# A gated layer's output phase in another order of blocks, its mixes one product later, the next rows' splits later

## The chip, the cores and the metric

The program runs on one core of a Trainium2 chip, and the metric is the device time of one execution in microseconds. TensorE does the matrix products, VectorE (DVE) and ScalarE (ACT) the elementwise work, GpSimd (POOL) helps in the first layer, SyncE (SP) issues most DMA transfers.

## What is computed

A decoder trunk of two layers on x (1 x 2048 x 1024, float32). Layer 0 is a hybrid of dilated sliding-window and differential attention; the change leaves it as it is. Layer 1 is a chunked gated MLP:

```python
def sgu_layer(x, norm_g, w_in, ln_g, ln_b, w_s, b_s, w_out):
    h = rms_norm(x, norm_g)                       # 2048 x 1024
    u, v, g = split(h @ w_in)                     # three times 2048 columns
    u = gelu(u)
    v = layer_norm(gelu(v), ln_g, ln_b)
    # in each 128-row chunk n and each of 8 column groups: causal 128 x 128 product
    sp = einsum('gts,bnsgc->bntgc', tril(w_s), chunks(v)) + b_s
    y = u * sp * silu(g)
    return x + y @ w_out                          # 2048 x 2048 by 2048 x 1024
```

## The kernel before

The 16 chunks of 128 rows ("blocks") of layer 1 go through in four groups `gi` of four. A group's blocks 0 to 3 are taken as two rows j = 0, 1 by two row halves r (block j + 2r). Every projection is a Strassen-like scheme (`strassen`, L915): seven products for j = 0 and j = 1 each, 14 steps n, and each step is twelve matmuls of 128x512 (L925): four slices of the inner dimension by three terms, since each float32 operand is held as a high and a low part in the faster float32r format. The helper `split` (L91, L92) makes these parts: ScalarE copies the high part, VectorE subtracts to get the low one. All such splits of weights (`w`), rows (`h`), mixed rows and turned rows (both `vs`) have line L92.

A group runs so:

1. v (m = 1) for both column halves `cc`, with GELU and the statistics of the layer norm.
2. For each `cc`: u (m = 0). During its steps the `mix` generators are called, eight of them, one for each row, row half r and column half c. The first call normalises a piece of v and splits it (`vs`, a ring of four); the second does the spatial products, six matmuls (L1095 to L1097) into a bank of `pp` (there are two), and ScalarE adds the bias into `vv`. u's own product with it waits in the list `pend`.
3. Then the gate g (m = 2). `g_done` (L1126) makes the gated columns: tanh on ScalarE (L1129), two operations on VectorE (L1130, L1131); L1131 writes them into `vv`.
4. Then the output phase (L1150 on): 16 output products M0 to M15 over (c, h, block), where h is a half of the 1024 output columns. `turned(b, c)` (L1133) transposes four 128x128 tiles (L1137) into `pp` and splits them into `vs`; twelve matmuls (L1168 to L1170) use them in one of three accumulator banks `y`; VectorE adds the bank to `acc` (L1171), and in the second column half the sum goes out.

Weights come in through `slot` (L860): SyncE loads a raw tile `wr` (a ring of three), which is split into one of five `w2` tiles. Some tiles of u's products (`k` 1 and 3) are split once, stored, and loaded again in the groups behind by L867 (`ws`).

While the output phase of `cc == 1` runs, the next group's rows are prepared (`rows_sums`, L962): a load of four row tiles into `hr` (one buffer, L969), then splits and sums (L979 to L995) for block pair 0 (j = 0), then, with the same buffer, for pair 1. Beside the output products of group 0, `cc == 0`, `turn` (L1000) finishes the last two blocks of layer 0, with transposes into the same `pp` (its multiply is L1014).

What sets the order: TensorE's instructions stand in the order in which the program is written. The other engines' instructions are ordered by a list scheduler that simulates the program; each engine then takes them in that order. So the place of a call in the text decides TensorE's order, and elsewhere only what the scheduler makes of it.

Of the kernel before, what the change touches and what calls it, by code (L numbers as in the profile page):

```python
# [60 lines left out]
def _trunk(tc, a, out):  # L61
# [3 lines left out]
    with ExitStack() as top:  # L65
# [760 lines left out]
        with ExitStack() as st:  # L826
            w1 = st.enter_context(tc.tile_pool(name="D_w", bufs=1, reuse_waits="tile"))
            ps = st.enter_context(tc.tile_pool(name="D_ps", bufs=1, space=PSUM, reuse_waits="tile"))
            NG, GB = 4, 4
# [5 lines left out]
            def tile_(shape, dt, tag, bufs):  # L835
                got = ahead.pop(tag, None)
                return w1.tile(shape, dt, name=tag, tag=tag, bufs=bufs) if got is None else got

            def psum(tag, shape, bufs):
                got = ahead_ps.pop(tag, None)  # L840
                return ps.tile(shape, F32, name=tag, tag=tag, bufs=bufs) if got is None else got
# [73 lines left out]
            def strassen(ht, m, cc, sum_to, done):  # L915


                x, y, u2, o = {}, {}, {}, {}

                def product(j, acc, i, w, start):  # L920

                    z = ht[j][i]
                    for kc in range(4):
                        for k, (p, q) in enumerate(((0, 0), (0, 1), (1, 0))):
                            T.matmul(acc, z[:, p, kc], w[kc][q], start=start and kc == k == 0, stop=kc == 3 and k == 2,  # L925
                                     skip_group_check=True)

                def taken(j, r, c, p):
                    o[j] = sum_to(j, r, c)
                    A.copy(o[j], p)  # L930

                def summed(j, r, c, p, q=None):
                    z = sum_to(j, r, c) if q is not None else o[j]
                    V.tensor_add(z, p, z if q is None else q)
                    done(j, r, c, z)

                for n, (i, *which) in enumerate(PRODUCTS):
                    w = quarter(m, cc, *which)
                    for j in range(2):
                        if n == 0:  # L940
                            x[j] = psum("x", [P, 512], 3)
                        elif n in (1, 3):
                            y[j] = psum("y", [P, 512], 3)
                        product(j, x[j] if n in (0, 2, 4, 6) else y[j], i, w, n in (0, 1, 3))
                        if n == 0:
                            taken(j, 0, 0, x[j])
                        elif n == 1:
                            summed(j, 0, 0, y[j])
                        elif n == 2:
                            u2[j] = tile_([P, 512], F32, "u2", 2)  # L950
                            A.copy(u2[j], x[j])
                        elif n == 3:
                            taken(j, 1, 1, y[j])
                        elif n == 4:
                            summed(j, 1, 1, x[j])
                        elif n == 5:
                            summed(j, 0, 1, y[j], u2[j])
                        elif n == 6:
                            done(j, 1, 0, x[j])
                        yield  # L960
# [63 lines left out]
            for g in rows:  # L1024
                next(g)
            for gi in range(NG):
                blocks = range(GB * gi, GB * gi + GB)
                vv, st6, acc = {}, {}, {}
                ht = ready.pop(gi)
                for b in blocks:  # L1030
# [6 lines left out]
                def columns(cc, c):  # L1037
                    return slice(512 * cc + 1024 * c, 512 * cc + 1024 * c + 512)
# [32 lines left out]
                for cc in range(2):  # L1071
# [43 lines left out]
                    mixes = [mix(*z) for z in order]  # L1115
                    pend = []
                    for n, _ in enumerate(strassen(ht, 0, cc, new_sum, u_done)):
                        if 3 <= n < 11:
                            next(mixes[n - 3], None)
                        if 1 <= n < 9:  # L1120
                            next(mixes[n - 1])
                        while pend and pend[0][0] <= n - 3:
                            pend.pop(0)[1]()


# [7 lines left out]
                    def turned(b, c):  # L1133
                        pt = psum("pp", [P, 512], 2).rearrange("p (c t) -> p c t", t=P)
                        s0 = columns(cc, c).start
                        for i in range(4):
                            T.transpose(pt[:, i], vv[b][:, s0 + P * i:s0 + P * i + P], ident)  # L1137
                        yT = tile_([P, 2, 512], F32R, "vs", VS_BUFS).rearrange("p k (c t) -> p k c t", t=P)
                        split(yT[:, 0], yT[:, 1], pt)
                        return yT  # L1140

                    for n, _ in enumerate(strassen(ht, 2, cc, new_sum, g_done)):
                        if n == 12:
                            nxt = turned(blocks[0], 0)

                    todo = iter(())
                    if cc == 1 and gi + 1 < NG:
                        ready[gi + 1] = []
                        todo = steps([rows_sums(gi + 1, j) for j in range(2)])
                    seq = [(c, h, b) for c in range(2) for h in range(2) for b in blocks]  # L1150
                    yT = {blocks[0]: nxt}
                    for n, (c, h, b) in enumerate(seq):
                        es = slice(512 * h, 512 * h + 512)
                        if n % GB == 0:
                            k0 = columns(cc, c).start // P
                            wo2 = []
                            for k in range(0, 4, 2):
                                wo2 += slot(wout[:, k0 + k:k0 + k + 2, es], 2)

                        if n + 1 < len(seq) and seq[n + 1][1] == 0:  # L1160
                            yT[seq[n + 1][2]] = turned(seq[n + 1][2], seq[n + 1][0])
                        if cc == 0 and c == h == 0:
                            acc[b] = tile_([P, D], F32, "acc", GB)
                            with tc.issue_after(urgent.ins):
                                nc.sync.dma_start(acc[b], x1_s[b])
                        po = psum("y", [P, 512], 3)
                        for i in range(4):
                            T.matmul(po, yT[b][:, 0, i], wo2[i][0], start=i == 0, stop=False)  # L1168
                            T.matmul(po, yT[b][:, 0, i], wo2[i][1], start=False, stop=False)  # L1169
                            T.matmul(po, yT[b][:, 1, i], wo2[i][0], start=False, stop=i == 3)  # L1170
                        V.tensor_add(acc[b][:, es], po, acc[b][:, es])  # L1171
                        if cc == 1 and c == 1:
                            nc.sync.dma_start(out[b * P:(b + 1) * P, es], acc[b][:, es])
                        if gi == 0 and cc == 0 and n in (6, 10):
                            turn(NB - LATE + n // 8)
                        next(todo, None)


def _host_constants():
# [56 lines left out]
```

## Time and profile before

| | |
|---|---|
| median of 3 runs | 3186.36 us (3172.94 to 3189.53) |
| profiled execution, and its span | 3193.26 us; 3191.5 us |
| mean granted TensorE clock | 0.979 of full |
| TensorE (PE) busy | 3001.6 us, 94% of the span |
| VectorE (DVE) busy | 2142.9 us, 67% |
| ScalarE (ACT) busy | 1641.5 us, 51% |
| GpSimd (POOL) busy | 726.6 us, 23%, none of it in the last half |

Layer 1 takes the last 1368 us of the span. A busy share is an average over stages that have different limits: what a change is worth in one stage is to be read from the waits in that stage. In rows of the trace a bracket such as `[1.34 <-DVE vs L92]` says that the engine stood idle 1.34 us before this instruction, until VectorE's instruction of line 92 on the tile `vs` was done; `x4` is a run of four like instructions, and the time before the engine's name is how long they took.

### The profile page before, as it was taken

To read this page: it belongs to the slowest core of one execution; us is meant where nothing else is said; L and a number is where in the kernel's file an instruction comes from. 1 tells how busy PE (TensorE), PEld (TensorE's weight loads), DVE (VectorE), ACT (ScalarE), POOL (GpSimd) and SP (SyncE) were. 2 spreads that over 40 slices of the span, in tenths; PEclk is the share of its full clock that TensorE was granted. 3 is DMA by queue.
4 is the path that set the end of the run, shared out by engine and by line. 5 is a ranking of instruction groups with operands and counts; after the bars stand their busy time and mean duration, and the time that the engine had idled before them with its cause. 6 is when DMAs were issued, how large, how long until landed. Compare 5 with 4: busy or idle time off the path is not lost.

```text
span 3191.5 us, 45535 instructions
## 1 busy us (share of the span) xinstructions
PE 3001.6 (94%) x15240; PEld 2508.5 (79%) x15240; DVE 2142.9 (67%) x4822; ACT 1641.5 (51%) x3012; POOL 726.6 (23%) x1855
## 2 busy tenths in 40 slices
PE   7879899998989999998999989999998999999999
PEld 6668787887878778887887778778887888777887
DVE  5436686457855677556886787757767677757765
ACT  5535555455545555554454664635554553645553
POOL 5535443445334543442123000000000000000000
PEclk9989999999999999999999999999999999999999
DMA  9987967878587876758437774647554664547553
GB/s 343 334 248 228 267 205 226 252 218 261 194 249 222 242 239 202 215 159 231 149 129 255 234 235 159 209 156 251 167 161 153 200 236 144 177 145 245 164 170 107
DMA packets 379915, 668.75 MB, mean 210 GB/s; under 512 B 61856, under 2 KB 176672, under 8 KB 375584
## 3 DMA queue, kind: packets, MB, share of 16 engines
q1 hardware_dynamic: 351648, 568.04, 57.9%
q0 software_dynamic: 27456, 95.70, 8.3%
q8 instruction: 120, 1.97, 0.3%
q10 hardware_dynamic: 576, 2.10, 0.2%
q14 instruction: 115, 0.94, 0.1%
HBM read 506.08 MB, written 134.48 MB: 201 GB/s over the span
## 4 chain that ended last, share of the span: by engine, by line
PE 72%; DMA 11%; DVE 9%; issue 3%; ACT 3%; POOL 1%; SPq 1%; DVEq 0%; ACTq 0%; POOLq 0%
PE x L925 14%; PE y L925 11%; PE pm L326 5%; PE pm L328 5%; PE pm L327 5%; PE pu L549 3%; PE y L1170 3%; PE y L1168 3%; PE y L1169 3%; PE po L645 3%; PE s_ps L506 3%; DMA hT<-hts 2%; DMA tq<-in_sgu_w_in 2%; PE pT L525 2%; PE sd_ps L608 1%
## 5 line engine op out<-in xcount | busy, mean ns | idle before, releaser
L92 DVE TENSOR_TENSOR w<-wr,w 128x1024 fp32r<-128x1024 f32 x376 | 459.3, 1222 | 240.2 <-ACT w L92 239.3
L925 PE MATMUL x<-w,h 128*128 128x512 f32 x2304 | 558.9, 397 | 9.7 <-DVE w L92 5.6
L925 PEld LDWEIGHTS x<-w,h 128*128 128x128 f32 x2304 | 434.1, 190 | 110.5 <-DVE w L92 8.2
L326 PE MATMUL pm<-wh,hT 128*128 128x512 f32 x1024 | 453.7, 443 | 69.0 <-DMA hT<-hts 51.1
L92 ACT CAST w<-wr 128x1024 fp32r<-128x1024 f32 x376 | 394.2, 1049 | 235.1 <-PE y L1170 89.8
L925 PE MATMUL y<-w,h 128*128 128x512 f32 x1728 | 414.1, 394 | 0.0
L327 PE MATMUL pm<-wl,hT 128*128 128x512 f32 x1024 | 410.6, 401 | 2.7 <-POOL wl L92 2.6
L328 PE MATMUL pm<-wh,hT 128*128 128x512 f32 x1024 | 411.9, 402 | 0.0
L925 PEld LDWEIGHTS y<-w,h 128*128 128x128 f32 x1728 | 323.3, 188 | 71.5
L326 PEld LDWEIGHTS pm<-wh,hT 128*128 128x128 f32 x1024 | 200.3, 196 | 92.5 <-issue 41.4
L615 ACT ACTIVATE sd<-sd,nmd 128x128 f32<-128x128 f32 (+15 forms) x128 | 153.9, 1203 | 165.8 <-DVE nmd L611 163.9
L328 PEld LDWEIGHTS pm<-wh,hT 128*128 128x128 f32 x1024 | 197.1, 192 | 46.2 <-DVE hT L217 1.2
L1170 PE MATMUL y<-w,vs 128*128 128x512 f32 x512 | 205.6, 401 | 11.8 <-DVE vs L92 11.7
L327 PEld LDWEIGHTS pm<-wl,hT 128*128 128x128 f32 x1024 | 199.9, 195 | 21.1 <-POOL wl L92 4.8
L1168 PE MATMUL y<-w,vs 128*128 128x512 f32 x512 | 209.7, 409 | 0.5 <-ACT vs L92 0.5
L1169 PE MATMUL y<-w,vs 128*128 128x512 f32 x512 | 204.3, 399 | 0.0
L517 ACT ACTIVATE sm<-sm,um 128x256 f32<-128x256 f32 (+1 forms) x256 | 115.5, 486 | 157.0 <-DVE um L515 156.8
L549 PEld LDWEIGHTS pu<-vt,pTs 128*128 128x128 f32 x1200 | 160.0, 192 | 22.3 <-ACT um L552 5.5
L549 PE MATMUL pu<-vt,pTs 128*128 128x65 f32 x1200 | 156.5, 268 | 6.3 <-ACT um L552 3.5
L515 DVE CUSTOM_DVE_ANT_0 sm<-s_ps,masks 128x256 f32<-128x256 f32 (+1 forms) x224 | 84.6, 415 | 110.8 <-PE s_ps L506 110.6
L645 PEld LDWEIGHTS po<-vd,pTds 128*128 128x128 f32 x1088 | 145.9, 192 | 15.0 <-ACT pTds L653 1.6
L1171 DVE TENSOR_TENSOR acc<-y,acc 128x512 f32<-128x512 f32 x128 | 88.2, 689 | 94.0 <-PE y L1170 92.6
(220 smaller groups left out, 5855.8 us busy)
## 6 DMA issues: line engine op xcount, KB each, us to landing
hT<-hts SPq DMA_DIRECT2D x224, 512.0 KB, 4.5
wr<-t SPq DMA_DIRECT2D x168, 512.0 KB, 4.3
wr<-in_sgu_w_in SPq DMA_DIRECT2D x144, 512.0 KB, 4.4
wr<-in_sgu_w_out SPq DMA_DIRECT2D x64, 512.0 KB, 3.9
tq<-in_sgu_w_in SPq DMA_DIRECT2D x96, 256.0 KB, 4.2
t<-tq POOLq DMA_DIRECT2D x48, 512.0 KB, 4.9
w<-ws SPq DMA_DIRECT2D x24, 1024.0 KB, 5.8
hts<-hT SPq DMA_DIRECT2D x32, 512.0 KB, 7.1
```

The costliest lines, as they stand in the source:

```text
L92: return A.copy(hi, src), E.tensor_sub(lo, src, hi.bitcast(F32))
L326: T.matmul(pm, z[:, 0, k], w[dc][0], start=dc == 0, stop=False)
L327: T.matmul(pm, z[:, 0, k], w[dc][1], start=False, stop=False)
L328: T.matmul(pm, z[:, 1, k], w[dc][0], start=False, stop=dc == DC - 1)
L517: A.activation(sm[:, t, :w], sm[:, t, :w], AF.Exp, bias=nm, scale=-1.0)
L549: T.matmul(pu[:, g0 % 4 + t], pTs[:, t, P * q:P * q + P], vt[pat][:, vb, 65 * i:65 * i + 65], start=q == 0, stop=q == nk - 1)
L615: A.activation(sm[:, :L], sm[:, :L], AF.Exp, bias=nm[:, nch - 1:nch], scale=-1.0, accum_out=lsum)
L645: T.matmul(po, pTs[:, k], v[:, k4 + k], start=k4 + k == 0, stop=k4 + k == i)
L925: T.matmul(acc, z[:, p, kc], w[kc][q], start=start and kc == k == 0, stop=kc == 3 and k == 2, skip_group_check=True)
L1168: T.matmul(po, yT[b][:, 0, i], wo2[i][0], start=i == 0, stop=False)
L1169: T.matmul(po, yT[b][:, 0, i], wo2[i][1], start=False, stop=False)
L1170: T.matmul(po, yT[b][:, 1, i], wo2[i][0], start=False, stop=i == 3)
```

## The change

Four things change in layer 1, and nothing in what is computed but the order in which float32 sums are added:

- The output phase takes the column halves as c = 1, 0 and the blocks as 2, 3, 0, 1. The stores of the second column half therefore go with c = 0.
- Its first two turned blocks are called at steps 12 and 13 of the gate's scheme; each later one after the add of the output product two places ahead of its own, where before it was called ahead of the matmuls of the product one place ahead.
- The spatial products of the mixes are called one step later (4 to 11 for 3 to 10), and so are the products in `pend`.
- The steps of the next group's rows are taken two at a time from n = 6 on, where before one was taken after each n.

```diff
-                        if 3 <= n < 11:
-                            next(mixes[n - 3], None)
+                        if 4 <= n < 12:
+                            next(mixes[n - 4], None)
                         if 1 <= n < 9:
                             next(mixes[n - 1])
-                        while pend and pend[0][0] <= n - 3:
+                        while pend and pend[0][0] <= n - 4:
                             pend.pop(0)[1]()
...
+                    yT = {}
                     for n, _ in enumerate(strassen(ht, 2, cc, new_sum, g_done)):
-                        if n == 12:
-                            nxt = turned(blocks[0], 0)
+                        if n >= 12:
+                            b = blocks[n - 10]
+                            yT[b] = turned(b, 1)
...
-                    seq = [(c, h, b) for c in range(2) for h in range(2) for b in blocks]
-                    yT = {blocks[0]: nxt}
+                    seq = [(c, h, b) for c in (1, 0) for h in range(2) for b in blocks[2:] + blocks[:2]]
...
-                        if n + 1 < len(seq) and seq[n + 1][1] == 0:
-                            yT[seq[n + 1][2]] = turned(seq[n + 1][2], seq[n + 1][0])
-                        if cc == 0 and c == h == 0:
+                        if cc == 0 and n < GB:
                             acc[b] = tile_([P, D], F32, "acc", GB)
...
                         V.tensor_add(acc[b][:, es], po, acc[b][:, es])
-                        if cc == 1 and c == 1:
+
+                        if n + 2 < len(seq) and seq[n + 2][1] == 0:
+                            yT[seq[n + 2][2]] = turned(seq[n + 2][2], seq[n + 2][0])
+                        if cc == 1 and c == 0:
                             nc.sync.dma_start(out[b * P:(b + 1) * P, es], acc[b][:, es])
                         if gi == 0 and cc == 0 and n in (6, 10):
                             turn(NB - LATE + n // 8)
-                        next(todo, None)
+                        if n > 5:
+                            next(todo, None)
+                            next(todo, None)
```

How this moves instructions, in three places. First TensorE, group 1, from the last gate products into the output phase of `cc == 1`, before (`vv_22623`, `22625`, `22627` and `22629` are the group's blocks 0 to 3; `L925` with `w_24897` and `w_24902` are the last two steps of the gate's scheme):

```order
L925 MATMUL x<-w_24897,h_22276 128x512 x6
L925 MATMUL x<-w_24902,h_22276 128x512 x6
L1137 MATMUL pp<-ident,vv_22623 128x128 x4
L925 MATMUL x<-w_24897,h_22416 128x512 x6
L925 MATMUL x<-w_24902,h_22416 128x512 x6
L1137 MATMUL pp<-ident,vv_22625 128x128 x4
L1168 MATMUL y<-w_24947,vs 128x512
...
L1137 MATMUL pp<-ident,vv_22627 128x128 x4
```

The same place in the changed kernel:

```order
L925 MATMUL x<-w_24897,h_22394 128x512 x6
L925 MATMUL x<-w_24902,h_22394 128x512 x6
L1137 MATMUL pp<-ident,vv_22627 128x128 x4
L925 MATMUL x<-w_24897,h_22502 128x512 x6
L925 MATMUL x<-w_24902,h_22502 128x512 x6
L1137 MATMUL pp<-ident,vv_22629 128x128 x4
L1167 MATMUL y<-w_24955,vs 128x512
...
L1137 MATMUL pp<-ident,vv_22623 128x128 x4
```

The transposes stand at the same places; the blocks in them are others. Next VectorE in the same phase, from the split of the second turned block on, before (`h` is the next group's rows; from `h_25122` on it is block pair 1):

```order
L92 TENSOR_TENSOR vs<-pp,vs 128x512
L1130 SCALAR_TENSOR_TENSOR th<-th,x 128x512
L92 TENSOR_TENSOR h_24987<-hr,h_24987 128x512
L1171 TENSOR_TENSOR acc<-y,acc 128x512
L1130 SCALAR_TENSOR_TENSOR th<-th,x 128x512
L1131 TENSOR_TENSOR vv_22627<-vv_22627,th 128x512
L1131 TENSOR_TENSOR vv_22629<-vv_22629,th 128x512
L92 TENSOR_TENSOR h_25122<-hr,h_25122 128x512
L92 TENSOR_TENSOR h_25123<-hr,h_25123 128x512
L986 TENSOR_TENSOR ct<-hr 128x512
L92 TENSOR_TENSOR vs<-pp,vs 128x512
```

And in the changed kernel (`h_25208` begins pair 1):

```order
L92 TENSOR_TENSOR vs<-pp,vs 128x512
L1130 SCALAR_TENSOR_TENSOR th<-th,x 128x512
L92 TENSOR_TENSOR h_25105<-hr,h_25105 128x512
L1130 SCALAR_TENSOR_TENSOR th<-th,x 128x512
L1170 TENSOR_TENSOR acc<-y,acc 128x512
L92 TENSOR_TENSOR vs<-pp,vs 128x512
L1131 TENSOR_TENSOR vv_22627<-vv_22627,th 128x512
L1131 TENSOR_TENSOR vv_22629<-vv_22629,th 128x512
L1170 TENSOR_TENSOR acc<-y,acc 128x512
L92 TENSOR_TENSOR vs<-pp,vs 128x512
L92 TENSOR_TENSOR h_25208<-hr,h_25208 128x512
L92 TENSOR_TENSOR h_25209<-hr,h_25209 128x512
```

Two splits of turned blocks and one more add now stand ahead of the first split of pair 1; the last split of pair 0 (`h_24987`, `h_25105`) stands where it stood. Last TensorE at the first mix of group 0 and `cc == 0`, before (`w_20501` and `w_20508` are the weights of step 4):

```order
L925 MATMUL y<-w_20440,h_19745 128x512 x6
L925 MATMUL y<-w_20445,h_19745 128x512 x6
L1095 MATMUL pp<-vs,wsp 128x256
L1096 MATMUL pp<-vs,wsp 128x256
L1097 MATMUL pp<-vs,wsp 128x256
...
L925 MATMUL x<-w_20501,h_19723 128x512 x6
L925 MATMUL x<-w_20508,h_19723 128x512 x6
```

And in the changed kernel:

```order
L925 MATMUL y<-w_20440,h_19745 128x512 x6
L925 MATMUL y<-w_20445,h_19745 128x512 x6
L925 MATMUL x<-w_20492,h_19723 128x512 x6
L925 MATMUL x<-w_20499,h_19723 128x512 x6
L1095 MATMUL pp<-vs,wsp 128x256
L1096 MATMUL pp<-vs,wsp 128x256
L1097 MATMUL pp<-vs,wsp 128x256
```

Step 4 of u's scheme has moved ahead of the first mix.

## Rows read from the trace of the kernel before

**Rows 1.** The head of the page.

```profile
span 3191.5 us, 45535 instructions
```

**Rows 2.** Waits of TensorE from 1824 us on: us in total, times, longest us.

```profile
PE pp L1137 <- DVE vv L1131: 17.3, 3, 5.8
PE y L1170 <- DVE vs L92: 11.7, 12, 1.7
PE pp L1096 <- DVE vs L92: 6.0, 4, 1.8
...
PE pp L1137 <- DVE th L1014: 0.5, 1, 0.5
```

**Rows 3.** Windows, second output phase, groups 0 to 3: us; busy (x) by engine (PE, PEld, DVE, ACT, POOL); clock.

```profile
2067.63:2101.48 33.85, 23.71 (x98) 17.91 (x97) 24.68 (x37) 11.22 (x18) 0.00 (x0) 0.90 0.40 135
2424.05:2457.32 33.27, 24.36 (x98) 18.53 (x97) 24.68 (x37) 11.22 (x18) 0.00 (x0) 0.90 0.41 139
2781.91:2814.93 33.02, 24.27 (x98) 18.84 (x97) 24.67 (x37) 11.31 (x18) 0.00 (x0) 0.90 0.33 107
3139.22:3160.69 21.47, 21.11 (x98) 16.94 (x96) 12.82 (x17) 5.29 (x7) 0.00 (x0) 1.00 0.16 56
```

**Rows 4.** Timeline of TensorE, group 1, that phase: start us, us, instruction [idle before <- releaser].

```profile
2426.46 0.50 PE L1170 MATMUL y<-w,vs 128*128 128x512 f32 x1 [1.34 <-DVE vs L92]
...
2428.66 0.40 PE L1170 MATMUL y<-w,vs 128*128 128x512 f32 x1
2434.82 1.09 PE L1137 MATMUL pp<-ident,vv 128*128 128x128 f32 x4 [5.76 <-DVE vv L1131]
...
2440.55 0.60 PE L1137 MATMUL pp<-ident,vv 128*128 128x128 f32 x4
```

**Rows 5.** Timeline of VectorE, the same stretch.

```profile
2423.91 0.69 DVE L1131 TENSOR_TENSOR vv<-vv,th 128x512 f32<-128x512 f32 x1
...
2429.85 1.23 DVE L92 TENSOR_TENSOR w<-wr,w 128x1024 fp32r<-128x1024 f32 x1
2430.99 0.69 DVE L92 TENSOR_TENSOR vs<-pp,vs 128x512 fp32r<-128x512 f32 x1
...
2432.18 0.70 DVE L92 TENSOR_TENSOR h<-hr,h 128x512 fp32r<-128x512 f32 x1
...
2433.98 1.30 DVE L1131 TENSOR_TENSOR vv<-vv,th 128x512 f32<-128x512 f32 x2
2439.13 1.29 DVE L92 TENSOR_TENSOR h<-hr,h 128x512 fp32r<-128x512 f32 x2 [3.85 <-ACT h L92]
```

**Rows 6.** Timeline of ScalarE, the same stretch.

```profile
2438.48 1.14 ACT L92 CAST h<-hr 128x512 fp32r<-128x512 f32 x2 [8.51 <-DMA hr<-h]
```

**Rows 7.** The two loads of `hr` for pair 1, group 1's phase (L969).

```profile
DMA to landing us min/median/max: 5.6/6.0/6.4
```

**Rows 8.** Timeline of TensorE, first spatial products of groups 0 and 1.

```profile
1856.37 0.58 PE L1095 MATMUL pp<-vs,wsp 128*128 128x256 f32 x1 [5.50 <-ACT vs L92]
...
1858.94 4.97 PE L925 MATMUL x<-w,h 128*128 128x512 f32 x12
...
2219.23 0.39 PE L1096 MATMUL pp<-vs,wsp 128*128 128x256 f32 x1 [1.74 <-DVE vs L92]
...
2219.92 2.94 PE L925 MATMUL x<-w,h 128*128 128x512 f32 x12
2222.70 0.28 PE L1095 MATMUL pp<-vs,wsp 128*128 128x256 f32 x1
```

**Rows 9.** Timeline of VectorE, a weight split before group 0's first mix.

```profile
1848.36 1.23 DVE L92 TENSOR_TENSOR w<-wr,w 128x1024 fp32r<-128x1024 f32 x1 [0.65 <-ACT w L92]
```

**Rows 10.** Loads of stored weights (L867): one in group 1, then all 24.

```profile
L867 SPq DMA_DIRECT2D w<-ws x1: 334/334/334, 2212.0 to 2212.0; - x1
...
DMA to landing us min/median/max: 8.7/8.7/8.7
...
DMA to landing us min/median/max: 4.8/5.8/9.1
```

More of the change, by code (lines that the diff above doesn't have):

```diff
@@ L1026, in _trunk @@
             for gi in range(NG):
-                blocks = range(GB * gi, GB * gi + GB)
+                blocks = list(range(GB * gi, GB * gi + GB))
                 vv, st6, acc = {}, {}, {}
```

## The prediction

> **What bounds the kernel now.** I read the page's head first, then the waits of TensorE in the second layer, then the four output phases as stretches, then one of them engine by engine. The profiled execution took 3193.26 us, 1.8 us more than its span [rows 1]; the median of the three runs is 3186.36 us (3172.94 to 3189.53). The change touches only the second layer; its waits I read from 1824 us on. The reader is to see that TensorE has no rival there: it waits seldom, and what it waits for is VectorE, in three places: a transpose that waits for a gated column (L1137 for L1131: 17.3 us in 3 pieces), an output product that waits for the low half of its turned rows (L1170: 11.7 us in 12) and the first spatial product of a group (L1096: 6.0 us in 4) [rows 2].
>
> The three long waits lie in the output phase of the second column half (`cc == 1`) of groups 0, 1 and 2. The windows from the second transpose of such a phase to that of the ninth turned block are one piece of work each, 98 matmuls: 33.85, 33.27 and 33.02 us, against 21.47 us in group 3, which has no next group to split for [rows 3]. The granted clock is 0.90 in the first three, 1.00 in the last: the stall of 5.8 us is followed by matmuls at the lower level (1.2 GHz). So 100.14 - 3 x 21.47 = 35.7 us (1.1%) is all that these phases can give.
>
> Group 1 shows why. Before M0 (the first output product) can use its turned rows, VectorE is busy with the next group's rows, and M0's third matmul waits 1.34 us; its last one starts at 2428.66. Then the transpose of block 2 waits until 2434.82 [rows 4], since the gating of block 2's columns (L1131, two in a row from 2433.98) stands in VectorE's queue behind row splits [rows 5]. Block 2's columns of half c=0 are the last that the gate's Strassen product gives.
>
> **The change part by part.** *Order of blocks.* Now c=1 and blocks 2, 3, 0, 1 come first. The order of TensorE's rows in group 1 (section on the change) shows that the places are the same: a transpose stands one output product ahead of its use in both. "Two products ahead" therefore moves nothing on TensorE and I cost it at nothing; only which block is turned changes. The third transpose now needs block 0 of c=1, gated at 2423.91 [rows 5], so the wait for L1131 goes. In the phases of the first column half (`cc == 0`) no transpose waits for a gated column, and nothing on TensorE waits for `acc` [rows 2]; the new order, the loads of `acc` and the stores, which keep their places in the count, are costed at nothing there.
>
> What is late next, VectorE's rows there show: two splits of turned rows have passed the row splits (h) of block pair 1, which wait for a load. The rest of the listing ahead of them is as before: the scheduler had already put pair 0's splits ahead of the phase, and "late" moves only pair 1's.
>
> I follow this queue on before's clock. M0's wait stays (1.34, with refill 1.5 us). The second transpose's split still ends at 2430.99 + 0.69 = 2431.68. The third transpose now starts at 2428.9 and M1 0.4 later, so M1's third matmul, due at about 2429.85, waits 1.85 us. From there VectorE takes some 0.6 us a row [rows 5]: the third split ends at 2434.7, when M2 asks for it at about 2435.2; the fourth at 2437.1, M3 asks at 2437.9: no wait. Then VectorE stands until the load lands, as before: issued when the last split of pair 0 is done (2432.18 + 0.69), landed 5.6 us later, used at 2439.13 [rows 5 to 7]. Behind it stand the adds that free the three accumulator banks. Counting 0.6 us a row and 1.14 for a weight split on VectorE, and 2.8 us for twelve matmuls (2219.92 to 2222.70 [rows 8]), the add of M2 ends at 2441.7 (M5 needs that bank at 2442.9), M3's at 2445.3 (M6: 2445.7), M4's at 2449.5 (M7: 2448.9, so 0.6 us of wait). The clock I leave at its upper level, as after M0's wait. If it fell, M1's twelve matmuls would again take 5.0 us as before (to the transpose at 2440.55 [rows 4]) instead of 2.8: 6.6 us in all, inside the forecast's own range. A phase then costs 21.47 + 1.5 + 1.85 + 0.6 = 25.4 us; three save 100.1 - 76.3 = 23.9 us. Ends: 0 and 35.7.
>
> The Trainium skill, TensorE: Matmul & The Clock Gate, table of specifications, says that ScalarE's and VectorE's queues are strict FIFO, so that nothing passes a waiting split. The trace agrees: ScalarE stood 8.51 us at the split of `hr` [rows 6] with a turned block's split behind it. If rows could pass, the 0.6 us of each phase would go and the saving would be 25.7 us.
>
> *Mixes one product later.* In group 0 the first spatial product waited 5.50 us, and the Strassen product behind it took 4.97 us at the lower clock instead of 2.94 [rows 8]. The changed kernel does one product more (2219.92 to 2222.70: 2.8 us) before it; the last VectorE split of its weights began at 1848.36 [rows 9], before the wait, so it fits in. Saving 2.8 us, up to 4.8 with the clock; I take 3.6, nearer the first. In groups 1 to 3 the wait of 1.74 us goes, but the product put ahead needs two weight tiles that arrive by DMA: in group 1 the second was issued at 2212.0 and landed 8.7 us later, at 2220.7 [rows 10], and its six matmuls would now start at 2219.23 - 1.74 - 0.28 + 1.4 = 2218.6: 2.1 us of wait in place of 1.74. Those loads land in 4.8 to 9.1 us [rows 10]. Ends for the three: a saving of 5.2, and, all at 9.1, a loss of 2.3; I take 0.
>
> *The two late blocks of layer 0 (`turn`).* The first one's transposes now follow the next turned block's in the two banks of `pp`, and its second half waits for that split (an add, a multiply, the split: some 1.9 us) where before 0.5 us was waited [rows 2]. I take 1.0 us; ends 0 and 2.
>
> Sum: -23.9 - 3.6 + 0 + 1.0 = -26.5 us: 3193.3 becomes 3166.8, and the median 3186.4 becomes 3160.
>
> **The rivals.** *All of it goes* (each phase as group 3's, first mixes free): 35.7 + 4.8 + 5.2 = 45.7 us, 3141. Against it: VectorE is busy 24.7 us in those windows [rows 3], more than the 21.47 that it would have.
>
> *VectorE is the bound*: the window becomes its own work and its wait for the load, 24.7 + 3.85 [rows 3, 5] = 28.5 us; saving 14.5 + 3.6 - 1.0 = 17.1, 3169. For it: what VectorE does in such a window does not shrink with the change. Against it: part of that work may follow the window, since TensorE waits only for splits and banks.
>
> *The late row splits hold the banks.* If the `hr` loads take 9.1 us instead of 5.6, every add behind them is 3.5 us later, beyond all the slack above: 10.5 us lost, and with first mixes at their worst 2.3 more: saving 13.7, 3173. For it: these loads now share the queues with weight loads in another order. Against it: no row shows them that late, and their place right behind the freed `hr` tile is kept for pair 1.
>
> *Slower*: the four `vs` tiles are now all in flight during the mixes, and VectorE stands at a full ring. If each of the 4 x 2 x 8 = 64 mixes costs TensorE one such split, 0.69 us [rows 5], that is 44.2 - 26.5 = 17.7 us slower, 3204; it decides from 0.41 us a mix. Against it: TensorE's first mixes were the late ones, and waits for VectorE at later mixes are not among the 4 of L1096 [rows 2].
>
> **How the numbers follow.** Forecast 0.58 (own range 3148 to 3172), all of it 0.08, VectorE bound 0.10, banks 0.18, slower 0.06. A difference of 0.5% (16 us: 3170.4) is about what a measurement can tell. Faster: nearly all of the forecast (0.55), 0.08, half of VectorE's, a third of the banks': 0.73; slower 0.06; the rest 0.21. The range 3140 to 3178 leaves out the slower case and the tails of the outermost two.
>
> **What would show it.** Right: no wait of L1137 for L1131; windows of 24 to 26 us with clock near 1.00; M0 and M1 still waiting 1.3 and 1.9 us; in groups 1 to 3 a wait for a `ws` load at the product ahead of the first mix. Wrong: a wait of some us for banks (adds of L1170) or for `vs` in these phases, waits of L1095 beyond the first mix, or windows still above 30 us.

## The result, and the profile after

The changed kernel takes 3164.03 us (median of 10 runs, 3153.40 to 3173.49); the kernel before took 3186.53 us in 10 runs (3172.94 to 3193.33). The ratio is 0.9927, 95% interval 0.9908 to 0.9945: 22.5 us faster, where 26.5 were forecast (3160 us). The profiled execution fell from a span of 3191.5 to 3166.5 us. The table of waits of TensorE in layer 1 (us in total, times, longest) answers to [rows 1, 2]:

```profile
span 3166.5 us, 45513 instructions
...
PE y L1169 <- DVE vs L92: 11.0, 11, 1.8
PE x L925 <- DMA w<-ws: 7.7, 3, 2.9
PE pp L1095 <- ACT vs L92: 2.7, 1, 2.7
...
PE pp L1096 <- DVE vs L92: 1.4, 2, 1.0
PE pp L1012 <- DVE th L1014: 0.9, 1, 0.9
PE y L1167 <- DVE acc L1170: 0.6, 1, 0.6
```

The wait of L1137 for the gated columns (17.3 us) is gone. New is a wait of 7.7 us for stored weights (`ws`), of which a second profile of the same kernel has 4.6 us (below). L1169 is the line that was L1170. In this text T0, T1, ... are the transposes of a phase's turned blocks in their order, M0, M1, ... its output products. The windows of [rows 3], from T1 to T4, now read:

```profile
2064.62:2090.67 26.05, 22.96 (x98) 18.08 (x97) 24.39 (x37) 11.14 (x18) 0.00 (x0) 0.93 0.41 134
2414.95:2439.47 24.52, 21.43 (x98) 16.78 (x97) 22.02 (x34) 11.22 (x18) 0.00 (x0) 1.00 0.37 124
2766.06:2790.53 24.47, 21.37 (x98) 16.86 (x97) 23.59 (x36) 11.02 (x18) 0.00 (x0) 1.00 0.40 132
3114.06:3135.59 21.53, 21.18 (x97) 16.89 (x96) 12.81 (x17) 5.29 (x7) 0.00 (x0) 1.00 0.17 56
```

The three phases take 75.0 us in place of 100.1. (T4 is the fifth turned block, the one for the ninth product, ahead of M7; the prediction calls it the ninth turned block. The windows are the same.) Group 1 in detail, TensorE as in [rows 4]:

```profile
2417.33 0.50 PE L1169 MATMUL y<-w,vs 128*128 128x512 f32 x1 [1.31 <-DVE vs L92]
...
2419.77 0.60 PE L1137 MATMUL pp<-ident,vv 128*128 128x128 f32 x4
...
2422.61 0.50 PE L1169 MATMUL y<-w,vs 128*128 128x512 f32 x1 [1.77 <-DVE vs L92]
...
2425.05 0.60 PE L1137 MATMUL pp<-ident,vv 128*128 128x128 f32 x4
...
2439.47 0.60 PE L1137 MATMUL pp<-ident,vv 128*128 128x128 f32 x4
2440.68 0.50 PE L1167 MATMUL y<-w,vs 128*128 128x512 f32 x1 [0.62 <-DVE acc L1170]
```

T2 starts without a wait right behind M0; M1 then waits 1.77 us for the split of the second turned block, and T3 follows. T4 (2439.47) ends the window; M7's wait for an accumulator bank, 0.62 us, lies behind it. VectorE and ScalarE in that stretch, as in [rows 5, 6]:

```profile
2416.60 0.68 DVE L92 TENSOR_TENSOR vs<-pp,vs 128x512 fp32r<-128x512 f32 x1
...
2421.87 0.68 DVE L92 TENSOR_TENSOR vs<-pp,vs 128x512 fp32r<-128x512 f32 x1
...
2424.87 0.68 DVE L92 TENSOR_TENSOR vs<-pp,vs 128x512 fp32r<-128x512 f32 x1
2425.47 1.28 DVE L1131 TENSOR_TENSOR vv<-vv,th 128x512 f32<-128x512 f32 x2
...
2427.27 0.68 DVE L92 TENSOR_TENSOR vs<-pp,vs 128x512 fp32r<-128x512 f32 x1
2430.45 1.29 DVE L92 TENSOR_TENSOR h<-hr,h 128x512 fp32r<-128x512 f32 x2 [2.50 <-ACT h L92]
```

```profile
2425.69 0.59 ACT L92 CAST vs<-pp 128x512 fp32r<-128x512 f32 x1 [4.36 <-PE pp L1137]
2429.80 1.85 ACT L92 CAST h<-hr 128x512 fp32r<-128x512 f32 x3 [3.52 <-DMA hr<-h]
```

The gating of the last two blocks (2425.47) begins 10.5 us after T1, where before it began 9.9 us after it (2433.98, T1 at 2424.05): it comes no earlier in the phase, but nothing waits for it. The third and fourth split (2424.87, 2427.27) are done before pair 1's rows (`h<-hr`) make both engines stand for their load. At the first mixes, as in [rows 8], and for one stored tile, as in [rows 10] (its second row is from the chain of work, start and duration until landing):

```profile
1854.59 0.39 PE L1095 MATMUL pp<-vs,wsp 128*128 128x256 f32 x1 [2.70 <-ACT vs L92]
...
1857.16 5.13 PE L925 MATMUL x<-w,h 128*128 128x512 f32 x12
...
2211.23 1.67 PE L925 MATMUL x<-w,h 128*128 128x512 f32 x6 [2.51 <-DMA w<-ws]
```

```profile
2201.96 9.22 DMA w<-ws
```

**Where the 25.0 us of the span went**, by the starts of products and of T0 in both timelines of TensorE: 1.8 us ahead of the fourth step of group 0's u, up to which TensorE, VectorE, ScalarE and GpSimd take the same rows in the same order in both kernels, so that the change has no part in them; 1.6 us from there to the first T0 (the first mix of group 0); -0.3 us in the first output phase with `turn`; then from T0 of each `cc == 1` phase to the next group's first T0 6.3, 6.9 and 9.5 us, 22.6 in all; -0.6 us in the rest. The 22.6 us are the windows' 25.1 us, less 1.0 us outside them in the phases (nearly all of it M7's bank wait and what follows it), 1.0 us more in the first three steps of the next groups' u, which differ from profile to profile, and 2.5 us less in the mixes, where the wait for stored tiles (7.7 us) stands in place of three waits of 1.74 us.

### The profile page after: what moved, and what is told of

Same layout as the page of the kernel before. It is cut to its first block, busy times and chain, and to the rows that moved or that the text cites. A ratio compares the mean times of both kernels' runs of the same rounds, so it can differ in the third digit from the quotient of the medians.

```text
span 3166.5 us, 45513 instructions
## 1 busy us (share of the span) xinstructions
PE 2994.0 (95%) x15240; PEld 2502.4 (79%) x15240; DVE 2141.0 (68%) x4822; ACT 1638.9 (52%) x3012; POOL 724.9 (23%) x1855
## 4 chain that ended last, share of the span: by engine, by line
PE 68%; DMA 13%; DVE 10%; issue 4%; ACT 3%; SPq 1%; POOL 1%; ACTq 0%; DVEq 0%; POOLq 0%
PE x L925 13%; PE y L925 11%; PE pm L326 5%; PE pm L328 4%; PE pm L327 4%; PE y L1169 3%; PE pu L549 3%; PE y L1167 3%; PE y L1168 3%; PE s_ps L506 3%; PE po L645 3%; DMA hT<-hts 2%; DMA tq<-in_sgu_w_in 2%; PE pT L525 2%; DVE w L92 2%
## 5 line engine op out<-in xcount | busy, mean ns | idle before, releaser
L925 PE MATMUL x<-w,h 128*128 128x512 f32 x2304 | 560.4, 398 | 15.1 <-DMA w<-ws 7.7
L925 PEld LDWEIGHTS x<-w,h 128*128 128x128 f32 x2304 | 434.8, 190 | 116.5 <-DMA w<-ws 9.0
L925 PE MATMUL y<-w,h 128*128 128x512 f32 x1728 | 414.1, 394 | 0.0
L925 PEld LDWEIGHTS y<-w,h 128*128 128x128 f32 x1728 | 323.4, 189 | 71.4
L327 PEld LDWEIGHTS pm<-wl,hT 128*128 128x128 f32 x1024 | 199.8, 195 | 21.5 <-POOL wl L92 5.0
L1169 PE MATMUL y<-w,vs 128*128 128x512 f32 x512 | 204.2, 399 | 11.0 <-DVE vs L92 11.0
L645 PE MATMUL po<-vd,pTds 128*128 128x128 f32 x1088 | 147.1, 275 | 1.3 <-ACT pTds L653 1.3
```

Of the source, the lines that this page charges most:

```text
L327: T.matmul(pm, z[:, 0, k], w[dc][1], start=False, stop=False)
L645: T.matmul(po, pTs[:, k], v[:, k4 + k], start=k4 + k == 0, stop=k4 + k == i)
```

## Experiments

Layer 0 is the same in all kernels, and yet layer 1 begins at 1736.8 us in one profile and at 1763.9 us in another. So I also read from each profile how long layer 1 takes, from the first product's start (line L925) to the end of the last output product. All kernels, with the three windows T1 to T4 of groups 0 to 2:

| kernel | ratio to before (95%) | layer 1, us | windows, us |
|---|---|---|---|
| before | 1 | 1438.3 | 33.9, 33.3, 33.0 |
| changed | 0.9927 (0.9908 to 0.9945) | 1414.7 | 26.1, 24.5, 24.5 |
| changed, again | 0.9924 (0.9904 to 0.9945) | 1411.4 | 24.6, 24.6, 26.1 |
| order_alone | 0.9953 (0.9940 to 0.9966) | 1418.8 | 27.2, 28.6, 26.0 |
| c_first | 0.9971 (0.9958 to 0.9983) | 1424.1 | 21.7, 21.0, 23.1 |
| late_alone | 1.0002 (0.9991 to 1.0013) | 1434.6 | 32.1, 33.3, 34.2 |
| mix_alone | 1.0003 (0.9990 to 1.0016) | 1437.7 | 33.8, 33.3, 33.6 |
| order_two | 0.9925 (0.9903 to 0.9947) | 1412.0 | 26.1, 26.0, 24.6 |
| order_mix | 0.9929 (0.9910 to 0.9949) | 1415.5 | 26.1, 24.6, 24.6 |
| no_rows | 0.9881 (0.9863 to 0.9899) | 1398.2 | 21.5, 21.5, 21.5 |
| hold | 0.9907 (0.9891 to 0.9924) | 1406.1 | 22.7, 22.7, 22.7 |
| hold, again | 0.9909 (0.9890 to 0.9928) | 1407.8 | 22.7, 22.7, 22.7 |
| mix_g0 | 0.9929 (0.9915 to 0.9944) | 1417.6 | 26.0, 29.1, 26.1 |
| hold_ln_g0 | 0.9910 (0.9895 to 0.9924) | 1405.9 | 23.1, 23.1, 23.1 |

One profile of layer 1 repeats to some 4 us: the two of the changed kernel differ by 3.3 us, and late_alone, which turns out to run the rows of the kernel before, by 3.7 us from it. In the second profile of the changed kernel the wait for stored tiles is shorter than in the first (7.7 us):

```profile
PE x L925 <- DMA w<-ws: 4.6, 3, 2.0
```

**Each part alone.** The new order alone:

```diff
-                            nxt = turned(blocks[0], 0)
+                            nxt = turned(blocks[2], 1)
-                    seq = [(c, h, b) for c in range(2) for h in range(2) for b in blocks]
+                    seq = [(c, h, b) for c in (1, 0) for h in range(2) for b in blocks[2:] + blocks[:2]]
```

> The kernel before with the new order alone (c = 1, 0; blocks 2, 3, 0, 1; first turned block is block 2 of c=1). My theory: the order alone removes the three waits of L1137 for L1131 (17.3 us and the half clock behind them), so it carries the whole gain of the output phases: the stretch from the second to the ninth turned block takes 24.5 to 26 us in groups 0 to 2 (before 33 to 34, changed kernel 24.5 to 26), and the time is 23 us under before, ratio 0.993. The first mix of group 0 still waits 5.5 us. Rival: the late row splits carry it, since without them pair 1's splits (which wait for a load) would stand ahead of the turned rows' splits again: then the stretch is above 28 us and the time at most 12 us under before.

It carries 19.5 of the 23.6 us by which layer 1 got shorter, by the times 0.0047 of 0.0073 (the median is 12.3 us under before, where 23 were expected). The waits for L1131 are gone, but in groups 0 and 1 another has come; ScalarE and TensorE in group 1:

```profile
2431.53 1.14 ACT L92 CAST h<-hr 128x512 fp32r<-128x512 f32 x2 [8.02 <-DMA hr<-h]
2432.57 0.58 ACT L92 CAST vs<-pp 128x512 fp32r<-128x512 f32 x1
```

```profile
2433.20 0.50 PE L1168 MATMUL y<-w,vs 128*128 128x512 f32 x1 [1.19 <-ACT vs L92]
...
2434.73 0.50 PE L1170 MATMUL y<-w,vs 128*128 128x512 f32 x1 [0.79 <-DVE vs L92]
```

Pair 1's split waits 8.02 us for its load, and the split of a turned block (2432.57) stands behind it, so that a product begins 1.19 us late. So both expectations failed in part: the windows sum to 81.8 us, between 75 and 84. Something else in the change moves that split.

The late row steps alone:

```diff
-                        next(todo, None)
+                        if n > 5:
+                            next(todo, None)
+                            next(todo, None)
```

> The kernel before with the next rows' steps two at a time from the seventh output product on, nothing else. My theory: the scheduler already puts pair 0's splits ahead of the phase, so TensorE still waits three times for L1131 and the stretch from the second to the ninth turned block stays at 31 to 34 us; time within 6 us of before. Rival: the late splits free VectorE early in the phase, L1131 comes 4 us earlier, and each of the three phases gains 4 to 9 us: 3160 to 3174 us.

As my theory had it: three waits of L1137 for L1131 (17.3 us), windows as before. TensorE, VectorE and ScalarE take the same rows in the same order as in the kernel before, in the whole program: added to it, the late steps do nothing. No run adds them to the new order alone, but order_two (below) and the changed kernel, which differ in them and in the mixes, have the same rows in the same order in these phases on ScalarE, and on VectorE but for the place of one row (L1130) in group 1. It looks as if the scheduler places the rows by when they can run in its simulation, not by where they are written.

The mixes alone:

```diff
-                        if 3 <= n < 11:
-                            next(mixes[n - 3], None)
+                        if 4 <= n < 12:
+                            next(mixes[n - 4], None)
-                        while pend and pend[0][0] <= n - 3:
+                        while pend and pend[0][0] <= n - 4:
```

> The kernel before with the mixes and their pending products one step later, nothing else. My theory: the first mix of group 0 waits 2.7 us in place of 5.5, and groups 1 to 3 wait 2.2 to 2.9 us for a stored weight tile in place of 1.74 us for a split: -3.0 + 2.5 = -0.5 us, the same time as before within what can be measured. Rival: the later mixes are themselves worth 5 to 10 us (their 1.74 us waits go and nothing takes their place): 3176 to 3181 us.

Layer 1 is 0.6 us shorter, which is less than a profile repeats to, and the ratio is 1.0003: the same time, as expected. Group 0 waits 3.3 us for 5.5, and in groups 1 to 3 the stored tiles cost 4.8 us in three waits, about as much as the three of 1.74 us that went:

```profile
PE pp L1137 <- DVE vv L1131: 17.3, 3, 5.8
...
PE x L925 <- DMA w<-ws: 4.8, 3, 1.9
PE pp L1095 <- ACT vs L92: 3.3, 1, 3.3
```

**Half of the new order:** c = 1 first, blocks still 0 to 3.

```diff
-                            nxt = turned(blocks[0], 0)
+                            nxt = turned(blocks[0], 1)
-                    seq = [(c, h, b) for c in range(2) for h in range(2) for b in blocks]
+                    seq = [(c, h, b) for c in (1, 0) for h in range(2) for b in blocks]
```

> The kernel before with the column halves as c = 1, 0 but the blocks still 0, 1, 2, 3. Block 0 and 1 of c=1 come out of the gate's scheme at steps 10 and 11, just ahead of their transposes. My theory (the order must follow that of completion): the wait moves to the first two transposes, which wait for the gating of blocks 0 and 1: on before's clock it ended at 2424.6 and 2429.3 where the transposes were due at 2420.9 and 2424.1, so 3 to 5 us a phase come back ahead of or in the stretch, in the first column half's phases too where before had none: time 5 to 20 us above the kernel with the new order alone. Rival: taking the early half c = 1 first is all that matters, since VectorE gates block 0 in time; then it equals the kernel with the new order alone within 4 us.

The windows are the shortest but one, since the wait has moved ahead of them, to T0. It is there in the first column half too (the second row, group 1's `cc == 0` phase):

```profile
2420.28 1.11 PE L1137 MATMUL pp<-ident,vv 128*128 128x128 f32 x4 [3.62 <-DVE vv L1131]
...
2284.69 0.66 PE L1137 MATMUL pp<-ident,vv 128*128 128x128 f32 x4 [1.22 <-DVE vv L1131]
```

Eight such waits make 17.0 us, and layer 1 takes 5.3 us more than with the whole new order. So the wait goes only where the order follows that of completion, as the theory said. What that is worth is less sure: 5.3 us is near the low end of its 5 to 20 us, but the medians are only 2.2 us apart, within the rival's 4 us, and the intervals of the ratios overlap.

**What else moves the fourth split.** The new order with the turned blocks called two products ahead, and the new order with the later mixes:

```diff
+                        if n + 2 < len(seq) and seq[n + 2][1] == 0:
+                            yT[seq[n + 2][2]] = turned(seq[n + 2][2], seq[n + 2][0])
```

> The new order with the turned blocks called after the add of two products ahead (the place they have in the changed kernel); mixes and next rows as before. On TensorE this is the order of the run with the new order alone; on VectorE and ScalarE the split of the fourth turned block stands ahead of pair 1's row splits in groups 0 and 1 too, where with the new order alone it stood behind them. My theory: what the new order alone lacked is that split's place, so T0 to T4 takes 27.7 to 29.2 us in each of groups 0 to 2 (30.4, 31.8, 29.2 with the new order alone; 29.2, 27.7, 27.7 in the changed kernel), with no wait of L1167 or L1168 (a block's first matmul) for ScalarE's split: 3 to 6 us under the new order alone. Rival: the place does nothing, and the difference came from the clock: T0 to T4 stays at 30 to 32 us in groups 0 and 1.

> The new order with the mixes one step later; turned blocks called one product ahead, next rows as before. Here too the scheduler puts the fourth turned block's split ahead of pair 1's row splits, though nothing in the text of the phase says so. My theory: T0 to T4 is 27.7 to 29.2 us in groups 0 to 2 and the whole of layer 1 takes as long as in the changed kernel within 2 us (1414.7 us from its first product to its last): the call two products ahead and the late row steps are then needed for nothing. Rival: without the call two products ahead the fourth block is late: T0 to T4 30 to 32 us.

In both the scheduler puts the fourth turned block's split ahead of pair 1's rows in every group, and both are as fast as the whole change. ScalarE in group 1 of order_two:

```profile
2418.65 0.58 ACT L92 CAST vs<-pp 128x512 fp32r<-128x512 f32 x1 [5.92 <-PE pp L1137]
2421.17 1.85 ACT L92 CAST h<-hr 128x512 fp32r<-128x512 f32 x3 [1.94 <-DMA hr<-h]
```

The split comes first and the wait for the load behind it. What that is worth has to be read at like clocks. Two windows of order_alone (groups 0 and 1), then two of order_two (groups 1 and 2):

```profile
2066.77:2093.96 27.19, 21.91 (x97) 16.68 (x96) 24.39 (x37) 10.92 (x18) 0.00 (x0) 1.00 0.40 131
2416.97:2445.53 28.56, 23.48 (x98) 17.87 (x97) 24.38 (x37) 10.92 (x18) 0.00 (x0) 0.94 0.36 115
...
2406.36:2432.40 26.04, 22.94 (x98) 17.98 (x97) 23.67 (x36) 11.19 (x18) 0.00 (x0) 0.93 0.40 124
2755.86:2780.41 24.55, 21.44 (x97) 16.80 (x96) 23.68 (x36) 11.11 (x18) 0.00 (x0) 1.00 0.41 133
```

In group 1 it is 28.56 against 26.04 us at granted clocks 0.94 and 0.93, in group 0 27.19 us against the 24.55 us that order_two takes at 1.00 in group 2: 2.5 and 2.6 us. In group 2 order_alone has the split ahead too, and its 26.04 us at 0.93 are order_two's time at that clock. So the call two products ahead, which changes nothing on TensorE in these phases (over the whole program it moves one turned block's four transposes ahead of `turn`'s), is worth some 5 us next to the new order alone; of the 6.8 us of layer 1 (1418.8 to 1412.0) another 2.3 us lie at the first mix of group 0, whose place in these two kernels is the same. The times agree but don't settle it (0.9925 and 0.9953, intervals that overlap). The later mixes move the split as well, and next to them the call is worth nothing (order_mix). Why an edit so far away moves it is not shown; that it shifts the scheduler's simulated times and so turns a close choice is a guess. order_two, without the later mixes and their waits for stored tiles, lies between the changed kernel's two profiles. The reverse shows in mix_g0, the changed kernel with `lag = 4 if gi == 0 else 3` for the mixes:

> The changed kernel with the mixes one step later in group 0 alone (in groups 1 to 3 at the old place). My theory: in groups 1 to 3 the waits for stored weights (2.5, 2.9 and 2.3 us) go and the old 1.74 us waits of L1096 for a split come back: -2.5 us, which the profile's waits show and the times hardly do (3161 to 3164). Rival: the tile also arrives too late for the step behind, so the wait for it stays beside the 1.74 us: +2 to +5 us.

The waits for stored tiles go and those of L1096 come back (6.4 us in 5), as expected; but in group 1 the scheduler put pair 1's rows ahead again, and the window grew to 29.1 us, 3 us more than the other two at the same granted clock (26.0 and 26.1 at 0.93). The gain of 2.5 us that was expected is gone: the ratio is the changed kernel's (the median of 3169.7 us was taken where before takes 3192.3):

```profile
PE pp L1096 <- DVE vs L92: 6.4, 5, 1.8
PE pp L1095 <- ACT vs L92: 3.0, 1, 3.0
PE y L1168 <- ACT vs L92: 1.8, 1, 1.8
```

**What is left in the phases.** The next groups' rows left out (`ready[gi + 1] = ht`):

> The changed kernel without the next group's rows: groups 1 to 3 take the rows of group 0 again, so their loads, splits and sums are left out (its output is that of group 0's rows). My theory: the waits that the changed kernel still has in these phases (M0 1.3 us, M1 1.8 us, M7 up to 0.6 us, half clock in group 0) come from VectorE's and ScalarE's work for the next rows; without it the stretch from the second transpose to that of the ninth output product takes 21.5 us in groups 0 to 2 as in group 3 (75.0 us becomes 64.5): 3152 to 3155 us. Rival: M0's and M1's waits come from the gating of blocks 2 and 3 (L1131) and the weight splits that stand there too, so the stretch stays at 24 us or more and the time within 4 us of the changed kernel.

The windows fall to 21.5 us and layer 1 by 13.2 to 16.5 us against the two profiles of the changed kernel:

```profile
2407.69:2429.20 21.51, 21.16 (x97) 16.88 (x96) 12.79 (x17) 5.30 (x7) 0.00 (x0) 1.00 0.34 107
```

VectorE's 12.79 us are group 3's. TensorE's waits for turned splits fall to 2.8 us in all of layer 1, none over 0.4 us. So what M0 and M1 still wait in the changed kernel comes from the rows, all but that remainder, and not from gating or weights. Holding the rows back then keeps the work and moves it:

```diff
-                            next(todo, None)
-                            next(todo, None)
+                            with ExitStack() as behind:
+                                for z in marks[1]:          # the second turned block's split
+                                    behind.enter_context(tc.issue_after(z.ins))
+                                next(todo, None)
+                                next(todo, None)
```

> The changed kernel with all of the next rows' splits and sums held on VectorE and ScalarE behind the split of the second turned block. My theory: the splits of the first two turned blocks then pass seven row instructions of 0.6 us, M0's wait falls to 0.4 us or less as in group 3 and M1's goes (1.3 + 1.8 us become 0.4), three times: -8 us, 3156. Rival: VectorE has no room (22 to 24 us busy in a stretch of 24.5), so the held work pushes the adds back and TensorE waits for accumulator banks (adds of acc) for 2 to 4 us a phase instead: no gain, 3160 to 3168.

> The changed kernel with the next rows' work held behind the second turned block's split, once more, on the chip of the run ahead. My theory: layer 1 is 8.7 us shorter than in the changed kernel (1406.0 against 1414.7 in the first profiles), so the ratio to before is 0.0025 to 0.003 below the changed kernel's. Rival: the gain was that profile's alone, and the ratios agree within 0.001.

> The changed kernel once more, beside the next run. Every theory: ratio to before 0.992 to 0.994, T0 to T4 27.7 to 29.2 us in groups 0 to 2.

Group 1's window, and all waits over 0.3 us from M0 to the phase's end in it, with T2 and T3:

```profile
2405.82:2428.51 22.69, 21.69 (x97) 16.72 (x96) 21.85 (x33) 11.72 (x18) 0.00 (x0) 1.00 0.42 147
```

```profile
2409.06 0.60 PE L1137 MATMUL pp<-ident,vv 128*128 128x128 f32 x4
...
2410.46 0.50 PE L1169 MATMUL y<-w,vs 128*128 128x512 f32 x1 [0.35 <-DVE vs L92]
...
2412.89 0.60 PE L1137 MATMUL pp<-ident,vv 128*128 128x128 f32 x4
...
2417.67 0.50 PE L1169 MATMUL y<-w,vs 128*128 128x512 f32 x1 [0.54 <-DVE vs L92]
...
2436.96 0.50 PE L1169 MATMUL y<-w,vs 128*128 128x512 f32 x1 [0.92 <-DVE vs L92]
```

M0, ahead of T2, does not wait at all; the 0.35 us are M1's, between T2 and T3, as in group 3 (the expectation puts them at M0). The windows are 22.7 us in all six phases of the two profiles, 7 us less for the three than in the changed kernel. But 3 us of that come back behind T4, where M9 waits 0.92 us in group 1 (0.9 to 1.2 us in all six phases) for a split that stands behind row and weight splits on VectorE: from T0 to the next group's first product the three phases take 162.2 and 162.4 us, against 166.3 and 166.5 in the changed kernel's two profiles. So 4 us stay of the 8 expected. Layer 1 takes 1406.1 and 1407.8 us against 1414.7 and 1411.4, more than those 4 us, by stretches that differ from profile to profile; the 8.7 us expected of the second round were 3.6. The ratios are 0.0020 and 0.0015 lower, with overlapping intervals, so the times alone don't settle it. Median 3159.5 us beside 3164.5 us on the same chip: the best version found. Last, the same with pair 1 held behind the fourth turned block, its rows loaded early into two tiles that are free by then, and the mixes as in mix_g0:

> The changed kernel with three edits: the next rows' work held behind the split of the second turned block (pair 0) and of the fourth (pair 1); pair 1's rows loaded into the two tiles of the layer norm's scale and shift, which are free by then, so that their load waits for nothing; and the mixes later in group 0 alone. My theory: M0 and M1 gain 8 us, the stand of VectorE for pair 1's load (1.4 to 2.5 us a phase) and the bank wait go (1 us), the stored weights give 2.5 us: 11 us under the changed kernel, 3153. Rival (VectorE is full there): the waits move to the turned blocks of the second half of the stretch and to the banks, 2 to 4 us a phase; 3158 to 3166.

```profile
2413.83:2436.94 23.11, 21.70 (x97) 16.72 (x96) 23.11 (x36) 12.35 (x20) 0.00 (x0) 1.00 0.27 82
```

```profile
PE y L1175 <- DVE acc L1178: 0.8, 1, 0.8
PE y L1177 <- DVE vs L92: 0.7, 2, 0.3
```

The rival was nearer: with its load early VectorE no longer stands at all, 23.11 of 23.11 us, and by the ratios the kernel is some 5 us under the changed kernel, where my theory had 11. TensorE waits 0.8 us for a bank and 0.7 us for splits in group 1's phase (the second block of rows), a little less than the 2 to 4 us of the rival. The early load drew more of VectorE's work into the stretch, 23.1 us for hold's 22.7; what it saved behind it (159.5 us from T0 to the next group's first product, for 162.2) doesn't show in layer 1 (1405.9 us) or in the ratio.

## Why the prediction was right, point by point

- **Order of blocks** (term -23.9, windows -25.1). The mechanism held. The walk along VectorE's queue held nearly row for row: M0's wait 1.31 us (forecast 1.34), M1's 1.77 (1.85), the bank wait of M7 0.62 (0.6), though in one group alone (group 1; group 0 in the second profile). c_first and order_alone show that the order is what removes the wait for L1131. That the sum came so near is in part luck. It counts M7's 0.6 us into a window that ends ahead of M7, and it adds M1's whole wait to group 3's 21.47 us, which hold 0.36 us of it already:

```profile
3142.45 0.60 PE L1137 MATMUL pp<-ident,vv 128*128 128x128 f32 x4
...
3143.88 0.51 PE L1170 MATMUL y<-w,vs 128*128 128x512 f32 x1 [0.36 <-DVE vs L92]
```

Without the two the forecast of a window is 24.5 us in place of 25.4, which is what two of the three took; the third took 26.05 us at a granted clock of 0.93, where the sum had left the clock at its upper level.

- **"Two products ahead moves nothing on TensorE and I cost it at nothing": this step failed.** The first half is so, but for four transposes beside `turn`, which have their own term; the second isn't, next to the new order alone, where order_alone and order_two price it at some 5 us of the windows. The order alone gets them to 81.8 us, not to the 75.0 that the prediction put down to it. The sum came out because I walked along the changed kernel's own order of rows, in which the split already had its place. In the changed kernel two edits put it there, the call and the later mixes, and either is enough; I priced neither for it.
- **"Late moves only pair 1's" splits: failed too.** It moves none (late_alone). The rival of the late splits that hold the banks fell with it; one bank wait of 0.6 us is all that is there.
- **First mix of group 0** (term -3.6, measured -1.6): this size was wrong by more than half. The wait fell by 2.8 us (5.50 to 2.70), but the half clock behind it stayed (twelve matmuls in 5.13 us, 4.97 before), which the value taken had partly counted as saved, and L1096 now waits 0.96 us for 0.76 and 0.47 us once more. (From u's fourth step to its thirteenth all profiles with the old place take 39.1 to 41.4 us, all with the later one 38.0 to 39.1.) The 1.8 us that the span gained ahead of it, in rows that the change leaves alone, made up for the miss: luck.
- **Mixes of groups 1 to 3** (term 0, measured +2.5 and, in the second profile, -0.5). The mechanism was named: the worked case, 2.1 us of wait, met 2.51 us, and that load landed in 9.22 us, near the 9.1 us at which the prediction put the worst end (+2.3). But the 7.7 us of three such waits are the first profile's alone. The second has 4.6 us, and five profiles of other kernels with later mixes in these groups have 3.8 to 4.8, no more than the 5.2 us that went.
- **`turn`** (term +1.0, measured +0.3): the wait for its multiply is 0.9 us in place of 0.5.
- **The rivals.** "All of it goes" needs the next rows gone (no_rows). "VectorE is the bound" is not so at 24.5 us, where VectorE stood 2.50 us for the load; but it is the next bound: in hold_ln_g0 it has no idle time in group 1's 23.1 us. The full ring of `vs` cost next to nothing: at L1096 TensorE waits 1.4 us in 2, both among the first three mixes of group 0.
- The Trainium skill, TensorE: Matmul & The Clock Gate, table of specifications, calls ScalarE's queue strictly in order. order_alone agrees: a turned block's split that had all its data stood behind a row split that waited 8.02 us.

## What to carry to other kernels

Consume results in the order in which the scheme completes them: here that took the longest waits out of three phases, and half of it (c_first) moved the wait ahead to T0 and kept only a part of the gain. When a scheduler orders some of the engines, read its rows and not the text: an edit that leaves the bound engine's order alone can move another engine's split past a wait for a load, and an edit that looks like a move may move nothing. Writing work later moved nothing here (late_alone); tying it behind an instruction that somebody waits for did (hold), and part of the gain came back as waits further on, so read the whole phase and not only the window.

## What the runs showed of the hardware

The same program lost the upper clock in one group in one execution and in another group in the next. With the same waits to 0.1 us the changed kernel's windows were 26.05, 24.52, 24.47 us at granted clocks 0.93, 1.00, 1.00 in one profile, and 24.58, 24.55, 26.09 us at 1.00, 1.00, 0.93 in the other. So the lower level (1.2 GHz), behind waits of 1.3 and 1.8 us, cost 1.5 us where it came; with waits of at most 0.56 us in the windows (hold) the clock was 1.00 in all six.
